# Latent attention after a dilated stage: where the heads' keys are loaded, who makes the branch pieces, when gates are stored, and the place of one copy

## The chip, the cores and the metric

The kernel runs on one core of one Trainium2 chip. The metric is the time of one execution on the device in microseconds (us); lower is better. Three runs of the kernel before gave 1240.01, 1243.35 and 1243.78 us, median 1243.35. One further execution was taken by the profiler: 1242.97 us, of which the span from the first to the last instruction is 1240.9.

## The reference

One layer of an encoder over 1024 tokens of width 1024, all in float32. Two mixers read one input projection, each is multiplied by SiLU of a branch of its own and projected, sigmoid gates weigh the two, and an output projection, a residual and a norm end it. Cut to what matters here:

```python
proj = rmsnorm(x, attn_norm_g) @ w_in     # c_q c_kv k_rope z_mla | q k v z_dil | g_mla g_dil
a_out = mla_attention(c_q, c_kv, k_rope, ...)        # 8 heads, dense, softmax over 1024 keys
y_mla = (a_out * silu(z_mla)) @ w_o_mla
d_out = dilated_mixture(q_dil, k_dil, v_dil, ...)    # 3 groups of 8 heads, dilations 1, 4, 16
y_dil = (d_out * silu(z_dil)) @ w_o_dil              # d_out: groups weighted by their softmax denominators
merged = sigmoid(g_mla + b) * y_mla + sigmoid(g_dil + b) * y_dil
out = rmsnorm(x + merged @ w_out)
```

## The kernel before

Every product of two float32 matrices is made from parts: an operand is split into a high part, rounded to the type fp32r, and a low part (the value less the high part), and three matmuls (`mm3`, lines 145 to 147: high by high, high by low, low by high) are summed. `split` (lines 151 and 152) rounds on ScalarE and subtracts on the engine that it is given, mostly GpSimd.

The program has five stages: the latent and value projections, the other projections of the dilated mixer (products of blocks), the dilated attention, the latent attention, and the output. In the last three the order of all instructions is written out by hand: every engine does its own in the order of the program, and waits by semaphores on the others. All DMAs go out through SyncE's queue (`dma`, line 141), in the program's order too: one that must wait holds up those behind it.

**Dilated attention** (`attention`). 72 units in a row, four pairs of heads with 16 units of the first two groups and 2 units of classes (the third group) each. In step t the units near t are each in another phase: scores, maxima, exponentials, transposes, values, copy, result. The last phase of a class unit (`result`, line 1255) copies its values from PSUM (tile `left`) to SBUF on VectorE. `combine` gives the steps that weigh the three groups of a pair: denominators go to DRAM and back by token, factors are made on GpSimd and VectorE (lines 1398 to 1419), stored (`s_rr`), and spread over 128 partitions by DMA (`spreads`, which uses the ring of buffers `bc`); lines 1441 and 1445 then multiply and add. For the last pair these steps fall into the first ticks of the latent attention (`LAST_STEPS`).

**Filler.** Beside all this TensorE computes the projections of the gates (`gate_fill`, 32 jobs of 8 steps, one `mm3` per step) and later those of the two branches (`proj_fill`). `feed(n)` adds n to what is owed and takes so many whole steps; in the dilated stage it is called twice per unit with `DIL_FEED`, by the group of the unit two ahead. After the last unit the steps are filled up to 224 of 256 in one go. The rest comes in the first 33 ticks of the latent attention, 2 per tick in two of four ticks. From `one_bank` on, a job has one PSUM bank.

A finished job goes through `after`: VectorE multiplies by a row factor (line 729), ScalarE takes tanh (line 735), and the tile (`zt`) joins the list `stores`; in the next jobs' third step (`kc == 2`) `store()` sends off one tile (`s_gt`). Its buffer, one of a small ring, can be written again when the store has landed. With two banks a tile joins the list after the next job's store, so it is sent a job later; this backlog of one stays when `one_bank` begins.

**Latent attention** (`mla_attention`). 32 units (head, quarter of the queries) of four ticks, c = 0 to 3. A tick transposes (line 871) the unit's exponentials, which ScalarE rounds (line 873) and VectorE subtracts (line 879). Ticks 0 and 1 make the next unit's scores (tiles `right`, `left`) and maxima (line 855); ticks 1 and 2 its exponentials (line 863). The values' matmuls (lines 895, 896) follow a tick behind; two units share a PSUM bank, whose halves ScalarE copies (line 902) and VectorE adds (line 911, `mla_sum`) before the next unit's values may write it.

At the end of every second unit of an odd head, `mla_spread` (tick c = 0) turns the denominators round (line 925), takes their reciprocals, stores them (`s_mr`) and reads them back spread over the partitions; `mla_gated` (line 941, GpSimd, tick c = 3) multiplies them into the branch's z, and `mla_weighted` (line 948, VectorE, the next unit's tick c = 1) applies both. The head after next has its queries and keys loaded (`mla_load_qk`: five DMAs, 1.5 MB, into one of two buffers each) in tick c = 1, as soon as the last scores of this head are issued, which is in the unit before its last.

`piece` makes the operands of the dilated branch's projection, eight pieces of 128 x 512 in ticks 6 to 32: the DMAs of z and of the summed dilated output y, `product` (line 1015, y = y * z on GpSimd) and a tick later `parts`, a `split` of y with the subtraction on GpSimd.

Some names are short in the profile: `at_r` and `at_f` are all tiles placed by hand (fp32r and float32), `bank` the PSUM banks, `w_h` and `w_l` the parts of weights, POOL is GpSimd, ACT ScalarE, DVE VectorE, PE TensorE, SPq SyncE's queue.

Of the kernel before, what the change touches and what calls it, by code (L numbers as in the profile page):

```python
# [10 lines left out]
F32 = mybir.dt.float32  # L11
# [3 lines left out]
ALU = mybir.AluOpType  # L15
# [13 lines left out]


FIRST_FEED = 9
DIL_FEED = (1.26, 1.26, 2.3, 1.8)

LAST_JOBS = [(dt, 0) for dt in range(4)] + [(dt + i, half) for dt in (4, 6) for half in range(2) for i in range(2)] + [(dt, 1) for dt in range(4)]
LAST_STEPS = {3: 4, 4: 6, 5: 8, 6: 9, 8: 14, 9: 15, 10: 17, 11: 19, 12: 20}
# [26 lines left out]
class Net:  # L62
# [656 lines left out]
    def gate_fill(self):  # L719
# [23 lines left out]
        for n, i in enumerate(ZG):  # L743
            w = self.split_weights.pop(n)
            for half in range(2):
                next(tail, None)
                ps = self.get("pj")
                t = slice(half * 512, half * 512 + 512)
                for kc in range(8):
                    self.mm3(ps, *self.at(w, kc), self.hTh[:, kc, t], self.hTl[:, kc, t], kc == 0, kc == 7)  # L750
                    if half == 0 and kc == 0:
                        self.weights_load(n + 2)
                    if half == 0 and kc == 4:
                        self.weights_split(n + 1)
                    if kc == 2:
                        store()
                    if kc % 2 and kc < 7:
                        next(tail, None)
                    if kc < 7:
                        yield  # L760
                run_all(tail)
                tail = after(2 * n + half, i, half, ps)
                if self.one_bank:
                    next(tail)
                yield True
# [193 lines left out]
    def mla_tick(self, k, c):  # L959

        self.mla_transposes(k, c)
        if c == 0:
            self.mla_low(k, c)
            self.mla_scores(k + 1, 0)
            self.mla_values(k - 1, 3)
            self.mla_copied(k - 1)
            self.mla_spread(k)
            self.mla_maxima(k + 1, 0)
            self.mla_sum(k - 1)
            h, u = self.units[k - 1] if k else (0, 0)  # L970
            if u == 3 and h < 6:
                self.mla_load_v(h + 2)
        elif c == 1:
            self.mla_exponentials(k + 1, 0)
            self.mla_low(k, c)
            self.mla_scores(k + 1, 1)
            self.mla_values(k, 0)
            self.mla_maxima(k + 1, 1)
            self.mla_weighted(k - 1)
            h, u = self.units[k + 1] if k + 1 < 32 else (7, 3)  # L980
            if u == 3 and h < 6:
                self.mla_load_qk(h + 2)
        else:
            if c == 2:
                self.mla_exponentials(k + 1, 1)
            self.mla_low(k, c)
            self.feed(self.rate)
            self.mla_values(k, c - 1)
            if c == 2:
                for n in {6: (), 7: (), 8: (5,), 9: (7,)}.get(k, (k - 1,)):  # L990
                    self.mla_merged(n, self.nc.gpsimd)
            else:
                self.mla_gated(k)

    def mla_attention(self, later, first):
# [5 lines left out]
        def piece(t, j, half, gap=5):  # L1001
# [10 lines left out]
                    o["y"] = self.last_sum[0][:, x]  # L1012

            def product():
                nc.gpsimd.tensor_tensor(out=o["y"], in0=o["y"], in1=o["z"], op=ALU.mult)

            def parts():
                self.split(o["y"], self.brd[0][j][half], self.brd[1][j][half], nc.gpsimd)
            put(t, load)
            put(t + gap, product)  # L1020
            put(t + gap + 1, parts)
# [281 lines left out]
    def attention(self):  # L1303
# [13 lines left out]
        for t in range(-2, N + 2):  # L1317
# [11 lines left out]
                self.mla_exponentials(0, t - N - 1) if t > N else None  # L1329
            self.feed(DIL_FEED[g])  # L1330
            do(t - 2, 6)
            do(t - 2, 7)
            if t == N + 1:
                self.places["s_mla"] = self.places["s_mla"] + self.banks_of("left", 1, S)
                self.mla_scores(0, 1)
# [4 lines left out]
            if t == N:  # L1340
# [3 lines left out]
                self.one_bank = True  # L1344
                self.places["s_mla"] = self.banks_of("right", 1, S)
                self.mla_scores(0, 0)
                self.mla_maxima(0, 0)
            if 1 <= t <= N:
                last = units[t - 1][-1]
# [388 lines left out]
```

## Time and profile before

| | |
|---|---|
| profiled execution, its span | 1242.97 us, 1240.9 us |
| median of three runs | 1243.35 us |
| TensorE matmul busy | 1206.6 us, 97% of the span |
| VectorE, ScalarE, GpSimd busy | 729.7, 616.0, 568.8 us |
| dilated attention | about 536 to 812 us of the span |
| latent attention | about 812 to 1112 us |

A row of the timeline gives the start from the span's first instruction, the duration, engine, line, operation, output and inputs, and in brackets how long the engine stood idle before it and what ended that. A row of the windows view gives for a stretch its length, then the busy time and number of instructions of PE, PE's weight loads, DVE, ACT and POOL, the granted TensorE clock, the DMA engines' share and GB/s. Other engines' idle time costs nothing as long as TensorE does not wait for them.

### The profile page before, as it was taken

Reading aid. Unit: us, or ns where it says so; the run is one execution under the profiler, and the core shown is the slowest. Engines: PE = TensorE matmul, PEld = TensorE weight load, DVE = VectorE, ACT = ScalarE, POOL = GpSimd, SP = SyncE. Lnnn points to the kernel's source line nnn. Section 1 sums busy time; section 2 is a strip of 40 time slices with the busy share of each in tenths; the row PEclk is TensorE's granted clock in tenths of the full one; section 3 lists DMA queues with packets and bytes.
Section 4 is the critical chain, followed back from the end, with each engine's and each line's share of the span. In section 5 each row is a group of like instructions: output and inputs, shape, how many; then the busy total and the mean of one; then the engine's idle time right before and its main releaser. Section 6 shows DMA issues by size and latency. Waiting matters only on the chain.

```text
span 1240.9 us, 19482 instructions
## 1 busy us (share of the span) xinstructions
PE 1206.6 (97%) x6909; PEld 1060.0 (85%) x6909; DVE 729.7 (59%) x1304; ACT 616.0 (50%) x1292; POOL 568.8 (46%) x482
## 2 busy tenths in 40 slices
PE   8989999999999999999999999999989999999997
PEld 8988999788888888888988888877878888888886
DVE  7473524466666663246566666556657767769542
ACT  7533345444343444456565656545655656654232
POOL 1361218777777777633465533415520201168322
PEclk9999999999999999999999999999999999999999
DMA  9858579365536643297889898946543445235241
GB/s 342 222 158 303 200 289 316 102 165 158 148 115 166 183 119 127 84 265 216 246 249 268 230 269 213 283 123 162 162 124 106 111 120 140 82 109 172 85 153 51
DMA packets 126416, 221.37 MB, mean 178 GB/s; under 512 B 28072, under 2 KB 60400, under 8 KB 121392
## 3 DMA queue, kind: packets, MB, share of 16 engines
q1 hardware_dynamic: 126320, 220.14, 59.8%
q8 instruction: 54, 0.88, 0.3%
q14 instruction: 42, 0.34, 0.1%
HBM read 149.24 MB, written 70.85 MB: 177 GB/s over the span
## 4 chain that ended last, share of the span: by engine, by line
PE 71%; DMA 9%; POOL 4%; issue 2%; ACT 2%; DVE 2%; SPq 1%; ACTq 0%; POOLq 0%; DVEq 0%
PE bank L145 6%; PE bank L146 6%; PE bank L147 6%; PE bank L871 3%; PE st_a L145 2%; PE st_a L147 2%; PE st_a L146 2%; PE st_d L145 2%; PE st_c L145 2%; PE st_d L147 2%; PE st_c L147 2%; PE st_c L146 2%; PE st_d L146 2%; PE bank L896 2%; PE right L145 2%
## 5 line engine op out<-in xcount | busy, mean ns | idle before, releaser
L152 POOL TENSOR_TENSOR w_l<-w_raw,w_h 128x512 fp32r<-128x512 f32 x188 | 246.1, 1322 | 231.0 <-ACT w_h L151 180.8
L151 ACT CAST w_h<-w_raw 128x512 fp32r<-128x512 f32 x188 | 112.1, 621 | 106.5 <-POOL w_raw L496 90.7
L145 PE MATMUL bank<-at_r,w_h 128*128 128x512 f32 x344 | 141.7, 412 | 0.0
L879 DVE TENSOR_TENSOR at_r<-bank,at_r 128x512 fp32r<-128x512 f32 x128 | 88.0, 688 | 82.6 <-ACT at_r L873 82.2
L146 PE MATMUL bank<-at_r,w_h 128*128 128x512 f32 x344 | 134.9, 392 | 0.6 <-POOL at_r L152 0.6
L147 PE MATMUL bank<-at_r,w_l 128*128 128x512 f32 x344 | 135.1, 393 | 0.0
L873 ACT CAST at_r<-bank 128x512 fp32r<-128x512 f32 x128 | 74.9, 586 | 75.5 <-PE bank L871 74.8
L145 PE MATMUL pj<-w_h,at_r 128*128 128x256 f32 x384 | 109.0, 284 | 0.2 <-ACT dv_s L457 0.2
L146 PE MATMUL pj<-w_l,at_r 128*128 128x256 f32 x384 | 108.9, 284 | 0.0
L147 PE MATMUL pj<-w_h,at_r 128*128 128x256 f32 x384 | 108.9, 284 | 0.0
L496 POOL TENSOR_TENSOR w_raw<-w_raw 128x512 f32<-128x512 f32 x64 | 82.9, 1295 | 0.1
L871 PE MATMUL bank<-consts,at_f 128*128 128x128 f32 x512 | 77.4, 273 | 1.6 <-ACT at_f L863 1.1
L147 PEld LDWEIGHTS bank<-at_r,w_l 128*128 128x128 f32 x344 | 64.7, 188 | 14.6
L1143 DVE TENSOR_TENSOR at_r<-bank,at_r 128x512 fp32r<-128x512 f32 x64 | 44.0, 688 | 54.4 <-ACT at_r L1139 54.2
L145 PEld LDWEIGHTS pj<-w_h,at_r 128*128 128x128 f32 x384 | 73.4, 191 | 1.3 <-ACT dv_s L457 0.6
L147 PEld LDWEIGHTS pj<-w_h,at_r 128*128 128x128 f32 x384 | 73.4, 191 | 1.0
L146 PEld LDWEIGHTS pj<-w_l,at_r 128*128 128x128 f32 x384 | 73.4, 191 | 0.7
L895 PE MATMUL bank<-at_r,at_r 128*128 128x256 f32 x256 | 67.7, 285 | 6.4 <-DVE at_f L911 3.3
L146 PEld LDWEIGHTS bank<-at_r,w_h 128*128 128x128 f32 x344 | 65.1, 189 | 9.7 <-POOL at_r L152 1.0
L145 PEld LDWEIGHTS bank<-at_r,w_h 128*128 128x128 f32 x344 | 65.1, 189 | 8.8
L896 PE MATMUL bank<-at_r,at_r 128*128 128x256 f32 x256 | 67.5, 285 | 0.9 <-DVE at_r L879 0.9
L1124 ACT ACTIVATE at_f<-at_f,at_f 128x256 f32<-128x256 f32 x128 | 64.1, 504 | 3.0 <-DVE at_f L1117 3.0
(323 smaller groups left out, 3321.6 us busy)
## 6 DMA issues: line engine op xcount, KB each, us to landing
w_raw<-wt SPq DMA_DIRECT2D x48, 512.0 KB, 4.2
at_r<-s_dq SPq DMA_DIRECT2D x32, 512.0 KB, 8.9
s_dk<-dq_st SPq DMA_DIRECT2D x80, 128.0 KB, 2.3
s_dv<-dv_st SPq DMA_DIRECT2D x32, 256.0 KB, 3.0
s_dq<-dq_st SPq DMA_DIRECT2D x64, 128.0 KB, 2.4
zt<-s_gt SPq DMA_DIRECT2D x32, 256.0 KB, 3.1
w_raw<-wv SPq DMA_DIRECT2D x12, 512.0 KB, 6.3
at_r<-s_dk SPq DMA_DIRECT2D x8, 576.0 KB, 10.1
```

The source lines that it names most:

```text
L145: mm(out, lh, rh, start=start, stop=False, skip_group_check=skip)
L146: mm(out, lh, rl, start=False, stop=False, skip_group_check=skip)
L147: return mm(out, ll, rh, start=False, stop=stop, skip_group_check=skip)
L151: self.nc.scalar.copy(out=h, in_=raw)
L152: sub.tensor_tensor(out=l, in0=raw, in1=h.bitcast(F32), op=ALU.subtract)
L496: self.nc.gpsimd.tensor_tensor(out=b[out], in0=b[x], in1=b[y], op=ALU.subtract)
L871: self.nc.tensor.transpose(pt[:, o:o + 128], self.P[k, b][:, 128 * kc:128 * kc + 128], self.ident)
L873: self.nc.scalar.copy(out=h, in_=pt)
L879: self.nc.vector.tensor_tensor(out=l, in0=pt, in1=h.bitcast(F32), op=ALU.subtract)
L895: mm(out, vv[:, kc], ph[:, x], start=kc == 0, stop=False)
L896: mm(out, vv[:, kc], pl[:, x], start=False, stop=kc == 7)
L1124: nc.scalar.activation(out=p, in_=p, func=AF.Exp, scale=-1.0, bias=nm, accum_out=den)
```

## The change

- `DIL_FEED` for the first two groups falls from 1.26 to 1.235.
- While a job has one bank, `store()` is also called in a job's sixth step (`kc == 5`).
- A head's queries and keys are loaded in tick c = 1 of the last unit of the head two before, one unit (four ticks) later; where that unit has an `mla_spread`, its DMAs now come first in the queue.
- A piece's high part is made by GpSimd: the product is computed twice, once into the fp32r operand and once in place, and the low part is the in-place product less the operand, in the next tick. ScalarE has no part in it.
- The last class unit's `result` moves from the step after the last unit, behind the first latent maxima, to the step before, between the first scores and the first maxima.

```diff
-DIL_FEED = (1.26, 1.26, 2.3, 1.8)
+DIL_FEED = (1.235, 1.235, 2.3, 1.8)
...
-                    if kc == 2:
+                    if kc == 2 or kc == 5 and self.one_bank:
                         store()
...
             self.mla_weighted(k - 1)
-            h, u = self.units[k + 1] if k + 1 < 32 else (7, 3)
+            h, u = self.units[k]
             if u == 3 and h < 6:
                 self.mla_load_qk(h + 2)
...
             def product():
-                nc.gpsimd.tensor_tensor(out=o["y"], in0=o["y"], in1=o["z"], op=ALU.mult)
+                for out in (self.brd[0][j][half], o["y"]):
+                    nc.gpsimd.tensor_tensor(out=out, in0=o["y"], in1=o["z"], op=ALU.mult)
 
             def parts():
-                self.split(o["y"], self.brd[0][j][half], self.brd[1][j][half], nc.gpsimd)
+                nc.gpsimd.tensor_tensor(out=self.brd[1][j][half], in0=o["y"], in1=self.brd[0][j][half].bitcast(F32), op=ALU.subtract)
...
             do(t - 2, 6)
-            do(t - 2, 7)
+            if t <= N:
+                do(t - 2, 7)
             if t == N + 1:
...
                 self.mla_scores(0, 0)
+                do(N - 1, 7)
                 self.mla_maxima(0, 0)
```

## The prediction

> **What bounds the kernel now.** I read the page first, then the busy time by stretches, then TensorE's waits and the timeline where it waits.
>
> ```profile
> span 1240.9 us, 19482 instructions
> PE 1206.6 (97%) x6909; PEld 1060.0 (85%) x6909; DVE 729.7 (59%) x1304; ACT 616.0 (50%) x1292; POOL 568.8 (46%) x482
> ```
> ```profile
> 536.00:800.00 264.00, 261.05 (x1661) 233.82 (x1660) 165.93 (x430) 157.67 (x421) 123.12 (x123) 1.00 0.89 247
> 800.00:835.00 35.00, 33.05 (x188) 28.16 (x187) 17.45 (x23) 15.10 (x27) 4.98 (x8) 1.00 0.55 156
> 835.00:870.00 35.00, 31.98 (x194) 27.77 (x194) 21.78 (x29) 19.69 (x36) 19.56 (x20) 1.00 0.61 153
> 870.00:910.00 40.00, 36.00 (x209) 30.33 (x208) 23.69 (x31) 22.79 (x41) 19.16 (x16) 0.98 0.54 156
> 910.00:1060.00 150.00, 150.00 (x926) 133.42 (x924) 108.29 (x139) 89.17 (x159) 20.49 (x16) 0.99 0.43 115
> ```
>
> TensorE is the bound: 1206.6 of 1240.9 us. The change removes no matmul, so it can only win what TensorE loses to waits. The second figure of a stretch, against the first, shows that: 2.95 us idle in nearly the whole dilated stage, none from 910 to 1060, but 1.95, 3.02 and 4.00 us in the 110 us between, where the latent attention begins and all five edits act. TensorE's waits in 800 to 912 name the releasers, and the timeline the places:
>
> ```profile
> PE bank L895 <- DVE at_f L911: 3.3, 3, 2.0
> PE bank L895 <- ACT at_r L873: 2.9, 1, 2.9
> PE bank L896 <- DVE at_r L879: 0.7, 2, 0.3
> ```
> ```profile
> 815.96 0.47 PE L145 MATMUL left<-at_r 96*128 96x512 f32 x1 [0.83 <-DVE at_f L1255]
> 820.21 0.55 PE L871 MATMUL bank<-consts,at_f 128*128 128x128 f32 x3 [1.12 <-ACT at_f L863]
> ...
> 840.37 0.60 PE L871 MATMUL bank<-consts,at_f 128*128 128x128 f32 x4
> ...
> 844.91 0.60 PE L871 MATMUL bank<-consts,at_f 128*128 128x128 f32 x4
> ...
> 861.02 0.60 PE L871 MATMUL bank<-consts,at_f 128*128 128x128 f32 x4
> ...
> 864.63 0.60 PE L871 MATMUL bank<-consts,at_f 128*128 128x128 f32 x4
> ```
> ```profile
> 903.43 0.60 PE L871 MATMUL bank<-consts,at_f 128*128 128x128 f32 x4
> ...
> 915.49 0.60 PE L871 MATMUL bank<-consts,at_f 128*128 128x128 f32 x4
> ```
>
> Line 871 opens a tick, so it is a clock for TensorE's progress. From 844.91 to 861.02 lie seven ticks: 16.11 / 7 = 2.30 us for a tick without a wait. By that measure tick 9 (840.37 to 844.91) loses 2.24 us, tick 17 (861.02 to 864.63) 1.31, ticks 18 to 33 (864.63 to 903.43, sixteen) 38.80 - 36.80 = 2.00, and ticks 34 to 36 (903.43 to 915.49) 12.06 - 6.90 = 5.16. Ahead of tick 1 come waits of 0.83 and 1.12 us. All of it: 12.66 us.
>
> The last 5.16 is more than the wait in it:
>
> ```profile
> 908.00:910.00 2.00, 1.34 (x5) 1.11 (x6) 1.67 (x2) 1.88 (x4) 0.41 (x1) 0.64 0.64 240
> 910.00:912.00 2.00, 2.00 (x9) 1.72 (x7) 1.35 (x3) 1.81 (x4) 0.02 (x1) 0.51 0.55 169
> ```
>
> The granted clock (third figure from the end) is 0.64 and 0.51 after the idle time; I price this stall by its ticks. The Trainium skill, "TensorE: Matmul & The Clock Gate", "What's actually happening", has the half clock come after an idle window of about 3.4 us; a wait of 2.9 us would by that keep the full clock, and the term would be 2.9 in place of 5.16. The trace differs, and the measurement decides.
>
> **The change, part by part.**
>
> *The last class result before the first maxima.*
>
> ```profile
> 813.66 1.23 DVE L855 TENSOR_REDUCE m_nm<-right 128x1 f32<-128x1024 f32 x1 [0.77 <-PE right L147]
> 814.81 1.01 DVE L1255 COPY at_f<-left 128x512 f32<-128x512 f32 x1
> 861.00 0.69 DVE L729 TENSOR_TENSOR zt<-bank,at_f 128x512 f32<-128x512 f32 x1 [2.58 <-DMA s_gt<-zt]
> ```
>
> The copy of 1.01 us ends at 815.82, and TensorE's scores into the bank that it frees start at 815.96. It stood behind the maximum of 813.66, before which VectorE was idle for 0.77 us waiting for scores. In front of that maximum the copy runs from 812.89 to 813.90, before TensorE asks at 815.13 (815.96 less its wait). The 0.83 us go. The maximum starts 0.24 us later, and with it an exponential on ScalarE; its reader comes only behind two stretches of filler, so this costs nothing.
>
> *Feed.* The steps of the dilated stage were 9 + 64 x 2.52 + 11 x 4.6 + 3.6 = 224, just the mark to which they are filled up; with 1.235 they are 9 + 64 x 2.47 + 11 x 4.6 + 3.6 = 221. So three steps go from the 64 units to the place right before the first tick. A step is three matmuls:
>
> ```profile
> 817.43 0.39 PE L145 MATMUL bank<-at_r,w_h 128*128 128x512 f32 x1
> 818.13 0.39 PE L145 MATMUL bank<-at_r,w_h 128*128 128x512 f32 x1
> ```
>
> 0.70 us each, 2.1 in all, in front of the wait of 1.12 us for the first exponentials: it goes. Cover is lost in the dilated stage, 0.03 us per unit, where TensorE's idle time is 2.95 us in 264. Bounds: if loads set the pace there (DMA engines 0.89 busy) all 2.1 us come back as waits; if the shifted jobs happen to close one of the waits, 0.8 us are won. I take 0.3, near the small end, as only three or four places wait at all.
>
> *Pieces on GpSimd alone.* In ticks 6 to 32 ScalarE, which rounds every tick's transposes, stood in its queue behind casts of pieces that waited for GpSimd:
>
> ```profile
> 840.73 0.62 ACT L151 CAST at_r<-zt 128x512 fp32r<-128x512 f32 x1 [3.35 <-POOL zt L1015]
> ...
> 906.45 0.62 ACT L151 CAST at_r<-zt 128x512 fp32r<-128x512 f32 x1 [5.08 <-POOL zt L1015]
> ```
> ```profile
> 839.42 1.28 POOL L1015 TENSOR_TENSOR zt<-zt,at_f 128x512 f32<-128x512 f32 x1
> ...
> 843.16 1.25 POOL L1015 TENSOR_TENSOR zt<-zt,at_f 128x512 f32<-128x512 f32 x1
> ...
> 903.90 1.29 POOL L941 TENSOR_TENSOR at_f<-at_f 128x512 f32<-128x512 f32 x1 [5.20 <-DMA at_f<-s_mr]
> ```
>
> The cast at 840.73 is the root of tick 9: the rounding (L873), VectorE's subtraction, a maximum and the sum L911 follow it in their queues, and TensorE's values wait for L911. The cast at 906.45 is the root of tick 34: it waited for a product that stood behind the gating L941, which waited for `s_mr`. Without the casts these 2.24 and 5.16 us go, and of the 2.00 in ticks 18 to 33, where the same casts and stores delay L879 and L911, I count 1.8 (two of these ticks hold one more transpose on TensorE, L925).
>
> Added are eight products of 1.28 us on GpSimd, 10.2 us, less eight casts of 0.62 us, 5.0 us, on ScalarE. GpSimd is busy 19.56 of 35 and 19.16 of 40 us there, so it has room; what counts is who stands behind. At 839 to 846 its operations are back to back, and behind them in SyncE's queue are the spreads of the last pair's factors, since they overwrite the buffers from which the second product reads:
>
> ```profile
> 844.44 3.65 SPq L141 DMA_DIRECT2D at_f<-s_rr  x6
> ...
> 851.39 0.34 SPq L141 DMA_DIRECT2D s_gt<-zt  x1
> ```
> ```profile
> 846.21 5.16 DMA at_f<-s_rr
> ```
> ```profile
> 856.05 1.28 DVE L1441 TENSOR_TENSOR at_f<-at_f 128x512 f32<-128x512 f32 x2
> ```
> ```profile
> DMA to landing us min/median/max: 2.3/6.0/11.5
> ```
>
> The last row is for another DMA, the last part of a head's keys (`s_kp`). Today the spreads start when that product ends (843.16 + 1.25), and the fourth has landed at 851.37, 4.68 us before its reader on VectorE at 856.05. Two more products come ahead of it (2.56 us), and TensorE's ticks, which set the reader's place, come 2.24 us sooner against GpSimd: 4.80 us of 4.68. So VectorE waits 0.1 us if the DMA takes 5.16 as now. Bounds: nothing, or, with that part's longest landing in place of 5.16, 6.3 us. I take 0.5, by the same DMA's own row.
>
> *Stores a job sooner.* The tile at 851.39 was sent a job late, behind the heads' load; VectorE waited for its landing until 861.00, and tick 17's 1.31 us are that. With the backlog gone the tile is sent some eight ticks earlier: the 1.31 go. The additional DMA issue on SyncE's queue, 0.34 us, only moves.
>
> *Keys behind the spread.*
>
> ```profile
> 886.45 0.45 SPq L141 DMA_DIRECT2D at_r<-s_qn  x1
> ...
> 893.16 0.29 SPq L141 DMA_DIRECT2D s_mr<-at_f  x1
> ...
> 900.39 1.09 SPq L141 DMA_DIRECT2D at_f<-s_mr  x2
> ```
>
> `s_mr` was issued at 893.16 behind a head's queries and keys, and its readers had to wait for its landing until 900.39. In the new order it is issued with the queue empty. This is the other half of tick 34 and adds no term, but it keeps VectorE's L948, which needs L941 too, from taking over the stall. A head's load then comes 15 ticks before its first scores, 7 for the last head:
>
> ```profile
> 1038.05 0.27 SPq L141 DMA_DIRECT2D s_mr<-at_f  x1
> ```
> ```profile
> 1053.05 0.47 PE L145 MATMUL right<-at_r 96*128 96x512 f32 x1
> ```
>
> Behind the spread of 1038.05, with its two readers and five issues of about half a microsecond, the last part is issued near 1042.5 (estimate from the rows' issue times) and, by the 6.0 and 11.5 above, lands at 1048.5 at the median, 1054 at the worst; it is needed at 1053.05. I take 0, bound 1.
>
> *Sum.* 0.83 + 1.12 + 2.24 + 1.31 + 1.8 + 5.16 = 12.46 us removed; 0.3 + 0.5 come back, and I keep 0.3 for small waits that no row shows. Gain 11.4: 1242.97 - 11.4 = 1231.6 for a profiled execution. The median of the runs is 0.38 above the profiled one, so 1232.0.
>
> **The rivals.**
>
> 1. *The spreads take the casts' place.* VectorE waits in tick 14 or 15 for a spread that lands as late as the bound, 6.3 us, of which TensorE, which uses VectorE's results a tick later, sees 6.3 - 2.3 = 4, and a microsecond more by the low clock. For: 4.80 against 4.68. Against: the same DMA took 5.16. Gain 11.4 - 5 = 6.4: 1237.
> 2. *VectorE keeps the stalls.* GpSimd's queue, longer by 10.2 us, delays L941 so that L948 on VectorE stands where the cast stood: the 5.16 from tick 34 on stay, 11.4 - 5.2 = 6.2: 1237. Against: GpSimd is half idle, and L941 waited for `s_mr`, not for work.
> 3. *GpSimd and VectorE block each other.* Six operations of VectorE with two inputs from SBUF (L1441 four times, L948 twice) fall among the added products; if each is held for one of 1.28 us, 7.7 us come back, 11.4 - 7.7 = 3.7: 1239.6. The row at 856.05 speaks against it: two of them took 0.64 each. By the Trainium skill, "SBUF — State Buffer", "SBUF: two separate sides", a two-input VectorE operation and a GpSimd operation lock a shared port against each other for a whole instruction, which would be this case; the trace of before shows no such hold in that row.
> 4. *No change.* The releasers that the profile infers are not the true ones, and the waits only move: 1243.
> 5. *Slower: the keys' burst.* Four heads' loads now come after the gates' loads of the second projection have begun, and push gate tiles and values behind them. If each costs TensorE a stall such as tick 34's, 11.4 - 4 x 5.16 = -9.2: 1252.6. It decides where a burst lands later than the work that needs it, for the last head beyond 10.5 us after issue. Against: the burst was in that stage before too, four ticks earlier, and 910 to 1060 has no idle time.
>
> **How the numbers follow.** Forecast 0.68 (1229.5 to 1235), rivals 1 to 5: 0.11, 0.07, 0.05, 0.05, 0.04. A measurement of this kernel tells about 0.3%, 3.7 us, from no change; forecast and rivals 1 and 2 are faster by more, rival 3 about half: 0.88. The rest of it and rival 4 are the same: 0.08; slower 0.04. The range: at the low end all 12.66 us and 0.8 of the feed go, 1243.35 - 13.46 = 1229.9, and I leave 0.4 below it, the distance of the profiled run from the median: 1229.5. At the high end rivals 1 and 2 are in: 1237.5.
>
> **What would show it.** Right: 800 to 910 with under 1 us idle in place of 8.97; line 871 every 2.30 us from tick 1 to 36; granted clock 1.00 throughout; no ScalarE cast of line 151 from `zt` or `at_f` before tick 34; `s_mr` read within 2 us of its issue. Wrong: L1441 waiting for `at_f<-s_rr` with TensorE behind it, a wait for `at_r<-s_kn` or `s_kp` near the last head's first scores, or new idle time before 800.

## The result, and the profile after

The kernel after took 1228.93 us in the median of six runs (1226.29 to 1231.00), the kernel before 1243.57 in six (1240.01 to 1248.18, the three named at the start among them): a ratio of 0.987, 95% interval 0.985 to 0.990. Its profiled execution took 1229.1 us, 13.9 us less than that of before, where 11.4 were forecast.

The first two lines of the page after, and the stretches that the prediction showed (columns as there):

```profile
span 1227.1 us, 19477 instructions
PE 1204.8 (98%) x6909; PEld 1061.2 (86%) x6909; DVE 729.4 (59%) x1304; ACT 611.9 (50%) x1284; POOL 579.1 (47%) x490
```
```profile
536.00:800.00 264.00, 263.41 (x1674) 235.69 (x1673) 167.18 (x433) 159.82 (x425) 122.92 (x123) 1.00 0.89 249
800.00:835.00 35.00, 35.00 (x204) 30.40 (x203) 19.32 (x25) 15.65 (x29) 9.90 (x14) 1.00 0.48 144
835.00:870.00 35.00, 34.99 (x214) 30.66 (x213) 24.23 (x31) 20.77 (x37) 22.40 (x20) 1.00 0.66 174
870.00:910.00 40.00, 38.83 (x237) 34.09 (x236) 27.31 (x36) 22.32 (x40) 24.96 (x20) 1.00 0.61 172
910.00:1060.00 150.00, 150.00 (x932) 133.44 (x931) 108.53 (x140) 88.70 (x158) 20.45 (x16) 1.00 0.42 108
```

TensorE's idle time from 800 to 910 is 1.18 us in place of 8.97. That was the forecast. The first row was not: 0.59 us idle in the dilated stage, where 2.95 were and a little more was expected.

The clock of line 871, from the timeline of after (first rows of some ticks):

```profile
816.85 0.60 PE L871 MATMUL bank<-consts,at_f 128*128 128x128 f32 x4
...
860.56 0.60 PE L871 MATMUL bank<-consts,at_f 128*128 128x128 f32 x4
863.27 0.66 PE L871 MATMUL bank<-consts,at_f 128*128 128x128 f32 x4
...
900.29 0.60 PE L871 MATMUL bank<-consts,at_f 128*128 128x128 f32 x4
904.03 0.60 PE L871 MATMUL bank<-consts,at_f 128*128 128x128 f32 x4
```

From tick 1 to the start of tick 37 are 83.44 us, 36 ticks of 2.30 and 0.64 of waits; before it were 93.51, so 10.07 us are gone. Two ticks are still long. Tick 20 (860.56 to 863.27) loses 0.41, tick 37 (900.29 to 904.03) 1.44. VectorE's and SyncE's rows of after show why:

```profile
861.32 0.69 DVE L1444 TENSOR_TENSOR at_f<-at_f,at_f 128x512 f32<-128x512 f32 x1 [3.21 <-DMA at_f<-s_rr]
...
902.23 0.69 DVE L811 SCALAR_TENSOR_TENSOR at_f<-zt,bank 128x512 f32<-128x512 f32 x1 [4.34 <-DMA zt<-s_gt]
```
```profile
885.36 0.31 SPq L141 DMA_DIRECT2D s_mr<-at_f  x1
887.88 1.09 SPq L141 DMA_DIRECT2D at_f<-s_mr  x2
889.07 0.55 SPq L141 DMA_DIRECT2D at_r<-s_qn  x1
...
891.24 0.58 SPq L141 DMA_DIRECT2D at_r<-s_kp  x1
...
892.99 9.88 SPq L141 DMA_DIRECT2D zt<-s_gt  x4
```

In tick 20 it is one of the last pair's spreads (the prediction's rival 1, at 0.41 of the 5 us that it feared). In tick 37 it is a gate tile that was asked for at 892.99, right behind a head's load of 1.5 MB, and read by line 811 at 902.23: rival 5, in one place of the four that it feared.

Of the signs that the prediction named for being right, three were narrowly missed: 1.18 us idle from 800 to 910 where under 1 was asked, a long tick 20 among the 36, and `s_mr` read 2.5 us behind its issue where 2 was asked.

Where the 13.8 us between the two spans (1240.9 and 1227.1) lie. The dilated stage is counted from its first score to the first line 871, the latent attention from there to its last:

| | before | after | difference |
|---|---|---|---|
| ahead of the dilated stage | 537.9 | 537.3 | -0.6 |
| dilated stage | 280.90 | 277.70 | -3.20 |
| latent attention | 293.24 | 283.26 | -9.98 |
| rest | 128.86 | 128.85 | 0 |

The first row is scatter: no instruction there is changed, and the profiled executions below have 533.1 to 540.5. It is also what makes single times of this kernel differ by several us, so that most of what follows is read from stages and ticks, and the runs' medians stand beside it.

### The profile page after: what moved, and what is told of

It reads as the page before. It is cut to its first block, busy times and chain, and to the rows that moved or that the text cites. A ratio compares the mean times of both kernels' runs of the same rounds, so it can differ in the third digit from the quotient of the medians.

```text
span 1227.1 us, 19477 instructions
## 1 busy us (share of the span) xinstructions
PE 1204.8 (98%) x6909; PEld 1061.2 (86%) x6909; DVE 729.4 (59%) x1304; ACT 611.9 (50%) x1284; POOL 579.1 (47%) x490
## 4 chain that ended last, share of the span: by engine, by line
PE 78%; DMA 9%; DVE 3%; ACT 3%; POOL 3%; issue 2%; SPq 1%; ACTq 0%; POOLq 0%; DVEq 0%
PE bank L145 6%; PE bank L147 6%; PE bank L146 6%; PE bank L871 4%; PE st_a L145 2%; PE st_a L147 2%; PE st_a L146 2%; PE st_c L146 2%; PE st_d L146 2%; PE st_d L145 2%; PE st_c L145 2%; PE st_d L147 2%; PE st_c L147 2%; PE bank L896 2%; PE bank L895 2%
```

## The experiments

A tick's loss is its length, from line 871 to line 871, less 2.30 us; those of before are in the prediction (tick 9 2.24, tick 17 1.31, ticks 18 to 33 2.00, ticks 34 to 36 5.16). The feed is 1.235 in a kernel that is made from after and 1.26 in one made from before, unless told otherwise. Ratios are to runs of the kernel before on the same chip.

### The feed

`feed_only` is the kernel before with

```diff
-DIL_FEED = (1.26, 1.26, 2.3, 1.8)
+DIL_FEED = (1.235, 1.235, 2.3, 1.8)
```

> The kernel before with the lower feed alone. Theory A (the feed shifts the filler against the DMA landings of the dilated stage and so closes waits there): the 1.12 us wait before the first tick goes and the idle time from 536 to 800 falls from 2.95 to about 0.6 us, 3.5 us less in all: about 1240 against 1243.6, with the 0.83 us wait for the last class copy and the stalls from tick 9 on unchanged. Theory B (those waits of the dilated stage come and go between executions, whatever the feed): only the 1.12 us go, about 1242.5, idle time from 536 to 800 anywhere between 0.5 and 3. Theory C (my prediction's term): the idle time there grows by 0.3 us, 1242.8.

1239.12 us, ratio 0.998 (0.996 to 1.000). Waits of 2.1 us are left in the dilated stage, 0.85 less than before, where theory A has 2.4 less. The ticks lose 11.5 us, without tick 17's but with 1.4 in tick 10: behind tick 9's wait of 1.94 us the granted clock was 0.50 for 3.4 us.

```profile
838.38:841.79 3.41, 3.41 (x14) 2.93 (x13) 2.38 (x3) 3.08 (x6) 1.27 (x1) 0.50 0.60 166
```

`all_but_feed` is the kernel after with

```diff
-DIL_FEED = (1.235, 1.235, 2.3, 1.8)
+DIL_FEED = (1.26, 1.26, 2.3, 1.8)
```

> The changed kernel with the feed of before. Theory A: the idle time from 536 to 800 is about 3 us again and the wait before the first tick returns, so 3.5 us above the changed kernel's 1228.9: 1232.4. Theory B: 1230.1, with an idle time from 536 to 800 that does not follow the feed. Theory C: 1229.7.

1233.53 us, ratio 0.994 (0.991 to 0.997). Waits of 3.38 us in the dilated stage, which lasts 282.66 us; the wait of 1.1 us before the first tick is back.

`first_feed_6` has that edit and three filler steps fewer ahead of the units, the old rate shifted:

```diff
-FIRST_FEED = 9
+FIRST_FEED = 6
```

> The changed kernel with the feed of before, but 6 instead of 9 steps ahead of the first unit: as many steps reach the place before the first tick, the units have the old cover each, and every job ends three steps later in the units, as it does near the end with the lower feed. If the place of the steps against the units decides (phase), the idle time from 536 to 800 is under 1 us and the time that of the changed kernel, 1228.9; if the smaller cover per unit decides, it is near 3 us and the time 1231.3. If the waits come and go by themselves it lies within 1 us of the changed kernel with an idle time that no pattern gives.

1236.04 us, ratio 0.995 (0.993 to 0.998). The shift takes away the two waits of 1.26 that are named below the table and brings others (1.55 us at 8 us from the stage's start, 0.62 at 115, 1.69 at 170): 5.27 us in all. So the waits changed places, as phase has it, but not to under 1 us, as the expectation had it. Behind the waits of 1.55 and 1.69 us the granted clock was 0.50 for 3.4 us each:

```profile
544.81:548.22 3.41, 3.41 (x9) 2.53 (x8) 1.37 (x5) 1.08 (x5) 3.22 (x3) 0.50 0.84 211
705.23:708.64 3.41, 3.41 (x12) 3.02 (x13) 1.63 (x7) 2.61 (x8) 1.41 (x2) 0.50 1.05 248
```

`feed_1245` and `feed_1225` are the kernel after with two other values:

```diff
-DIL_FEED = (1.235, 1.235, 2.3, 1.8)
+DIL_FEED = (1.245, 1.245, 2.3, 1.8)
...
-DIL_FEED = (1.235, 1.235, 2.3, 1.8)
+DIL_FEED = (1.225, 1.225, 2.3, 1.8)
```

> The kernel after with a feed of 1.245 in place of 1.235 (1.26 before). If the feed counts through the places at which gate jobs end against the units (phase), the waits in the dilated stage come and go with the value, in no order: with 1.245 some other places wait, between 0.5 and 3.5 us in all, and no wait of 0.75 us at 193 to 194 together with one of 1.5 us at 248 to 249 us behind the stage's start. If it counts through the amount (cover), 1.245 lies between 0.6 us (1.235) and 3 us (1.26) and waits at the same two places. Either way 1229 to 1232 us.

1229.6 us, ratio 0.988 (0.985 to 0.991); waits of 1.13 us in the dilated stage. Ticks 37 and 38 lose 3.7 us here (1.44 in after): TensorE's wait there was 1.85 us (1.17 in after), and the granted clock behind it 0.50 for 3.4 us (1.00 in after).

> The kernel after with a feed of 1.225 in place of 1.235. Four steps fewer than at 1.26 stand between the units, one or two more before the first tick. Phase: waits somewhere between 0.5 and 3.5 us in the dilated stage. Amount, with less better: 0.6 us or under, the time at or below that of 1.235. The prediction's view, by which less filler is less cover: 0.7 us or more. 1228 to 1232 us.

1234.47 us, ratio 0.992 (0.989 to 0.994); waits of 1.74 us, one of 1.37 us at 163, and 1.80 us more in the steps in front of the first tick, where TensorE waits for line 729 to clear the job's bank.

`feed_result` is the kernel before with two edits:

```diff
-DIL_FEED = (1.26, 1.26, 2.3, 1.8)
+DIL_FEED = (1.235, 1.235, 2.3, 1.8)
...
-            do(t - 2, 7)
+            if t <= N:
+                do(t - 2, 7)
...
                 self.mla_scores(0, 0)
+                do(N - 1, 7)
```

> The kernel before with two edits, the feed of 1.235 and the last class result in front of the first maxima. If the feed's value sets the waits in the dilated stage: under 1.2 us there, no wait of 0.75 us at 193 us or of 1.5 us at 248 us, none at the class copy, 1.12 us less before the first tick, and the ticks' 10 us of waits as in the kernel before: about 1243.4 - 2.4 - 0.8 - 1.1 = 1239 us. If they go with the execution: 1 to 4 us in the dilated stage at other places than in the run with the feed alone, and 1240 to 1242 us.

1237.6 us, ratio 0.994 (0.991 to 0.996): 0.36 us of waits in the dilated stage, none of the old ones. The ticks lose 11.7 us, 1.0 more than before.

Since no other edit touches the dilated stage, every kernel is an execution of it with its feed. Waits up to 262 us from its start, and its length:

| feed | executions | waits, us | length, us |
|---|---|---|---|
| 1.26 | 3 (before, `all_but_feed`, `pieces_only`) | 1.96 to 3.38 | 280.90 to 282.81 |
| 1.245 | 1 | 1.13 | 278.15 |
| 1.235 | 12 (after, and eleven below and above) | 0.35 to 2.10, ten under 1 | 276.37 to 280.55, eleven under 278.7 |
| 1.225 | 1 | 1.74 | 280.25 |

The lengths of 1.26 and 1.235 don't overlap, if only by 0.35 us (`feed_only` is the longest of 1.235), the waits only by one execution (again `feed_only`, which waits 1.06 us at 98 us from the stage's start, where the others have at most 0.46): the gain goes with the value. Two of the lengths at 1.26 include a low clock: behind the longer wait of the stage it was 0.50 for 3.4 us in `all_but_feed` and for 6.8 us in `pieces_only`, while it was 1.00 there in before and in all executions of 1.235. That the gain does not go with the amount is shown only in part: the one execution each of 1.245 and 1.225 waits more than ten of the twelve at 1.235, but less than the longest of them. It weighs more that `first_feed_6`, with the rate of 1.26 and its jobs shifted, waits at other places. At 1.26 TensorE waits 1.50 to 1.62 us at 246 to 249 us from the stage's start in all three, and 0.75 to 0.80 at 193 to 194 in two; at 1.235 no execution has over 0.36 us at the one or over 0.34 at the other. Here is the longer wait, ScalarE's rows and TensorE's, in before and in `all_but_feed`:

```profile
783.70 0.72 ACT L735 ACTIVATE zt<-zt,consts 128x512 f32<-128x512 f32 x1 [3.83 <-DVE zt L729]
784.33 0.57 ACT L1139 CAST at_r<-bank 128x512 fp32r<-128x512 f32 x1
784.79 0.51 ACT L1124 ACTIVATE at_f<-at_f,at_f 128x256 f32<-128x256 f32 x1
...
785.45 0.33 PE L1131 MATMUL bank<-consts,at_f 128*128 128x128 f32 x1 [1.50 <-ACT at_f L1124]
```
```profile
787.53 0.72 ACT L735 ACTIVATE zt<-zt,consts 128x512 f32<-128x512 f32 x1 [3.89 <-DVE zt L729]
788.16 0.57 ACT L1140 CAST at_r<-bank 128x512 fp32r<-128x512 f32 x1
788.62 0.51 ACT L1125 ACTIVATE at_f<-at_f,at_f 128x256 f32<-128x256 f32 x1
...
789.28 0.33 PE L1132 MATMUL bank<-consts,at_f 128*128 128x128 f32 x1 [1.62 <-ACT at_f L1125]
```

A gate job ends just there. Its tanh (line 735) waits 3.8 us for VectorE's line 729, and behind it in ScalarE's queue stand a rounding and the exponentials for which TensorE waits. In after (the same stretch, lines shifted by one):

```profile
779.82 0.51 ACT L1125 ACTIVATE at_f<-at_f,at_f 128x256 f32<-128x256 f32 x1 [1.24 <-DVE at_f L1118]
...
780.48 0.33 PE L1132 MATMUL bank<-consts,at_f 128*128 128x128 f32 x1 [0.26 <-ACT at_f L1125]
...
784.95 0.72 ACT L735 ACTIVATE zt<-zt,consts 128x512 f32<-128x512 f32 x1 [3.43 <-DVE zt L729]
```

The tanh still waits 3.43 us, but now behind the exponentials that TensorE needs first, which cost it 0.26. The value of the feed sets at which place of a unit a job ends. That the waits at these two places come and go with the value is shown by the runs; that the tanh in front makes the wait of 1.50 is read from the traces and was not tried by itself.

### The pieces

`all_but_pieces` is the kernel after with `product` and `parts` as before:

```diff
-                for out in (self.brd[0][j][half], o["y"]):
-                    nc.gpsimd.tensor_tensor(out=out, in0=o["y"], in1=o["z"], op=ALU.mult)
+                nc.gpsimd.tensor_tensor(out=o["y"], in0=o["y"], in1=o["z"], op=ALU.mult)
...
-                nc.gpsimd.tensor_tensor(out=self.brd[1][j][half], in0=o["y"], in1=self.brd[0][j][half].bitcast(F32), op=ALU.subtract)
+                self.split(o["y"], self.brd[0][j][half], self.brd[1][j][half], nc.gpsimd)
```

> The changed kernel with the pieces' high parts cast on ScalarE again. Measured from the first to the last tick in the profile (283.3 us in the changed kernel, 293.2 before), which leaves out the scatter of the earlier stages. Theory A (a cast stalls ScalarE only as long as GpSimd's product is late; with the keys behind the spread GpSimd no longer waits for s_mr): the stall of tick 9 returns (2.2 us) and some of ticks 25 to 27 (0.7 us), not that of tick 34: 286.2. Theory B (the casts alone make all three): 2.2 + 1.2 + 5.2 come back, 291.9.

1229.94 us, ratio 0.992 (0.988 to 0.995). Tick 9 loses 2.25 again and ticks 25 to 27 1.17, but tick 34 only 0.13: with the spread's read landed early, the product that the last casts wait for is early too. From the first to the last line 871 are 285.3 us, near theory A's 286.2 and 2.1 more than in after, which the medians can't show (tick 37 loses only 0.23 here).

`pieces_only` is the kernel before with the same lines the other way round, the change's edit of the pieces and nothing else.

> The kernel before with the pieces alone on GpSimd. Theory A: tick 9's 2.25 us and most of the 2.0 us in ticks 18 to 33 go, but tick 34 stays near its 4 us in another form, since the gating on GpSimd still waits for the spread behind the load and VectorE's product waits for that: 1243.4 - 4 = about 1239.5 us. Theory B (the casts are the root of tick 34, as the prediction had it): 1243.4 - 9.2 = 1234 us. For the feed of 1.26: waits of about 0.75 us at 193 to 194 us and 1.5 us at 248 to 249 us behind the stage's start if they go with the value, others or none if with the execution.

1246.05 us, ratio 1.001 (0.999 to 1.004): nothing is won, which neither theory had. Tick 9 is short and ticks 18 to 32 nearly all, as expected, but ticks 17 and 18 lose 8.2 us in place of 1.3, and 33 and 34 4.2, there too by line 729 behind a store (3.69 us at 906.29). SyncE's, VectorE's and TensorE's rows of `pieces_only`:

```profile
848.13 3.65 SPq L141 DMA_DIRECT2D at_f<-s_rr  x6
851.87 0.54 SPq L141 DMA_DIRECT2D at_r<-s_qn  x1
...
854.88 0.39 SPq L141 DMA_DIRECT2D s_gt<-zt  x1
```
```profile
864.07 0.69 DVE L729 TENSOR_TENSOR zt<-bank,at_f 128x512 f32<-128x512 f32 x1 [6.95 <-DMA s_gt<-zt]
...
867.13 0.58 PE L895 MATMUL bank<-at_r,at_r 128*128 128x256 f32 x1 [5.46 <-DVE at_f L911]
```

The spreads wait for GpSimd's second product and go out at 848.13 (844.44 before), the head's load behind them, and behind that the gate's store at 854.88 (851.39 before). Its landing frees the tile that line 729 writes, at 864.07 (861.00 before), while tick 17 begins sooner (859.7, before 861.02). In the kernel after no such wait is left, and undoing either the stores or the keys (below) doesn't bring it back: either of the two is enough here, and without both the pieces don't pay. Both take the store that line 729 needs out from behind the load. In `all_but_stores` it goes out just ahead of it:

```profile
840.30 0.58 SPq L141 DMA_DIRECT2D s_gt<-zt  x1
840.93 0.44 SPq L141 DMA_DIRECT2D at_r<-s_qn  x1
```

In `all_but_keys` a store still goes out behind the load (847.56, landed at 856.52), but line 729 runs at 849.06 without it: what it needs had been sent by 820.86.

Is it the cast on ScalarE that costs, or its wait for GpSimd? Three kernels keep the casts on ScalarE but two ticks later. `late_casts` is `all_but_pieces` with

```diff
-            put(t + gap + 1, parts)
+            put(t + gap + 3, parts)
```

In all three, some pieces are cast from a buffer that a later load has already filled again, so that the branch's projection gets other data; the work is of the same amount.

> The kernel after, with the pieces' high parts cast on ScalarE again as before, but two ticks later, so that GpSimd's product has long been made when the cast's turn comes. Theory A (what cost TensorE time was that the cast waited 3.35 to 5.08 us for GpSimd at the head of ScalarE's queue, not the cast itself): the eight casts of 0.62 us show waits of ScalarE well under 1 us, tick 9 stays under 0.2 us of excess, ticks 18 to 33 under 0.5 us in all, and the time is that of the kernel after, 1228 to 1231 us. Theory B (the 0.62 us on ScalarE is the cost, wherever it stands): 1 to 2 us of excess in the ticks of the casts, 1231 to 1233 us.

1235.79 us, ratio 0.994 (0.993 to 0.996). Up to tick 35 theory A holds: tick 9 loses nothing, ticks 18 to 33 lose 0.66, a little over the 0.5 expected. But ticks 36 and 37 lose 8.8: the last piece's cast stood 8.02 us in ScalarE's queue for a load of gates into its own buffer, which the edit itself put in front of it.

`late_casts_keys` has in addition the load of `keys_after_gates` (below).

> The casts on ScalarE two ticks later, and the load of head 3 behind the gates' loads (as in the run that put it there). With GpSimd's eight second products gone, the last pair's spreads are issued earlier, so that the wait of tick 20 (0.3 to 0.7 us) goes; with the load later, that of tick 37 (1.4 us) goes. If both hold and nothing else waits, the latent attention's ticks lose under 0.5 us in all and the time is 1.5 to 2 us under the kernel after: 1227 us. If the casts' 0.62 us on ScalarE show in the ticks, the gain is lost again: 1229 us or more.

1233.63 us, ratio 0.992 (0.990 to 0.995). Tick 20's wait is gone (0.11), ticks 36 to 38 lose 5.0 by the same cast (4.15 us in its queue).

`six_late_keys` is `late_casts_keys` with the last two pieces made by GpSimd alone, as in after, and in their old ticks:

```diff
-            put(t + gap + 3, parts)
+            put(t + gap + (3 if t < 24 else 1), parts)
```

> The kernel after, with the first six pieces' high parts cast on ScalarE two ticks later, the last two left on GpSimd, and head 3's load behind the gates' loads. Theory A (only the wait for GpSimd cost time, and GpSimd's second products delay the last pair's spreads): no excess over 0.5 us in any tick from 1 to 40, since tick 20's wait for a spread goes with the earlier issue and tick 37's for gates with the later load: 1.5 us under the kernel after, about 1227.5 us. Theory B (the cast costs by itself): 1 to 2 us of excess in ticks 9 to 28, 1229 us or more. For the feed: the dilated stage at 1.235 has under 1 us of waits if the waits go with the value, anything up to 4 us if they go with the execution.

1227.54 us, ratio 0.987 (0.984 to 0.989). The only ticks with a loss are 20, 25 and 28 (0.11, 0.43, 0.11): theory A. The time stands 1.4 us under that of after, within what the two sets of runs can tell apart.

`early_products` is `all_but_pieces` with the load of `keys_after_gates` and the products a tick earlier (for the last pair, j = 3, the casts a tick later), so that each cast comes two ticks behind its product and ahead of the load that takes its buffer:

```diff
-            put(t + gap, product)
-            put(t + gap + 1, parts)
+            put(t + gap - (j < 3), product)
+            put(t + gap + 1 + (j == 3), parts)
```

> The kernel after, with the pieces' high parts cast on ScalarE in the ticks of the kernel before, GpSimd's single product a tick earlier (for the last pair's two pieces the cast a tick later instead), and head 3's load behind the gates' loads. Theory A (only the wait at the head of ScalarE's queue cost time): the casts wait under 1 us, ticks 1 to 40 lose under 1.2 us in all, against 2.0 in the kernel after and 10.5 in the kernel before, and the time is 1 to 1.5 us under the kernel after, about 1227.5 us. Theory B (the casts cost by themselves, or the products in their new place delay the spreads as the second products did): 2 us or more in ticks 9 to 28, 1230 us or more.

1229.21 us, ratio 0.988 (0.985 to 0.991): no different from the kernel after. Tick 9 loses nothing, tick 26 1.53. ScalarE's rows of the second and the fifth piece:

```profile
837.20 0.62 ACT L151 CAST at_r<-zt 128x512 fp32r<-128x512 f32 x1 [0.85 <-POOL zt L1018]
...
876.42 0.62 ACT L151 CAST at_r<-zt 128x512 fp32r<-128x512 f32 x1 [3.16 <-POOL at_r L152]
```

Where the cast waits 0.85 us TensorE loses nothing; where it waits 3.16, until the end of a subtraction that stands behind the product and the gating in GpSimd's queue, the tick is long. It is the wait at the head of ScalarE's queue that costs, not the 0.62 us, but for a small rest: tick 25 loses 0.28 to 0.43 us in all eight kernels that cast pieces on ScalarE and nothing in the ten others, for a reason that no run shows. The forecast of at most 1.2 us for these ticks was missed by one cast (2.2 measured).

### The keys

`all_but_keys` is the kernel after with

```diff
-            h, u = self.units[k]
+            h, u = self.units[k + 1] if k + 1 < 32 else (7, 3)
```

> The changed kernel with a head's keys loaded in the unit before the last, as before. Theory A (as the prediction put it: without the casts the late s_mr stops VectorE's L948 instead, so the keys' place guards what the pieces won): L948 waits some 2 us in tick 33, TensorE 1 to 2 us behind it, while the 1.4 us of tick 37 go: 283 to 284.5 from the first to the last tick. Theory B (the keys' place is what ended the stall of tick 34): 5.2 us come back, 287 to 288.5. Theory C (the keys' place gives nothing): 281.9, faster than the changed kernel.

1233.63 us, ratio 0.993 (0.989 to 0.996). GpSimd's and VectorE's rows:

```profile
897.02 1.26 POOL L941 TENSOR_TENSOR at_f<-at_f 128x512 f32<-128x512 f32 x1 [10.93 <-DMA at_f<-s_mr]
...
898.32 1.73 DVE L948 TENSOR_TENSOR at_f<-at_f 128x512 f32<-128x512 f32 x1 [4.76 <-POOL at_f L941]
```

Ticks 35 and 36 lose 6.9 us, and from the first to the last line 871 are 289.1 us: theory A's mechanism, at more than theory B's size. The gating waits for the spread behind the load, and now VectorE's line 948 stands where ScalarE's cast stood: rival 2's mechanism, kept away by the keys. Of TensorE's one wait of 4.30 us there, 1.05 come from what held line 948 (last section), and the granted clock was 0.50 from 899.8 to 906.7.

`keys_after_gates` is the kernel after with head 3's load moved on, behind the gates' first loads:

```diff
-            if u == 3 and h < 6:
+            if u == 3 and h < 6 and h != 1:
                 self.mla_load_v(h + 2)
...
-            if u == 3 and h < 6:
+            if u == 3 and h < 6 and h != 1:
                 self.mla_load_qk(h + 2)
...
+            if k == 8 and c == 2:
+                self.mla_load_qk(3)
+                self.mla_load_v(3)
```

> The changed kernel with head 3's queries, keys and values loaded behind the first gate tiles of the second projection instead of in front of them (tick 34 instead of 29). If the new wait in tick 37 is the gate tile standing behind the head's load, VectorE's 4.3 us wait for it falls under 1 us and TensorE's 1.4 us in tick 37 go: 1227.5. If the gate tile is late for another reason (its buffer's store), nothing changes: 1228.9.

1229.68 us, ratio 0.989 (0.986 to 0.993). The stretch of tick 37's wait in after, and the same stretch in `keys_after_gates`:

```profile
902.00:904.00 2.00, 0.83 (x6) 0.51 (x5) 1.77 (x3) 0.00 (x0) 0.00 (x0) 1.00 0.54 205
```
```profile
902.00:904.00 2.00, 2.00 (x15) 1.78 (x14) 1.60 (x3) 1.52 (x3) 0.00 (x0) 1.00 1.12 287
```

Tick 37 loses nothing: the burst ahead of the gates' loads was its cause. The ticks gain 1.1 us, which the median of the runs can't show.

### The stores

`all_but_stores` is the kernel after with

```diff
-                    if kc == 2 or kc == 5 and self.one_bank:
+                    if kc == 2:
```

> The changed kernel without the second place of the stores. Theory A (the store was late because it stood behind the heads' load; with the load after it in the queue it lands in time): VectorE's wait for it in tick 15 is under 0.5 us and nothing comes back, 283.3 from the first to the last tick. Theory B (it is late by the job alone): the 1.3 us of tick 17 and the half microsecond of tick 33 come back, 285.1.

1232.96 us, ratio 0.993 (0.990 to 0.995). Tick 17 stays short, against the prediction's term. Ticks 37 and 38 lose 6.8 us instead, and from the first to the last line 871 are 288.7 us, which neither theory had. SyncE's and VectorE's rows:

```profile
887.25 0.43 SPq L141 DMA_DIRECT2D at_r<-s_mv  x1
887.78 1.15 SPq L141 DMA_DIRECT2D s_gt<-zt  x2
897.17 1.90 SPq L141 DMA_DIRECT2D zt<-s_gt  x4
```
```profile
899.83 0.69 DVE L811 SCALAR_TENSOR_TENSOR at_f<-zt,bank 128x512 f32<-128x512 f32 x1 [7.34 <-DMA zt<-s_gt]
```

The backlog's last two gate tiles go out together behind the head's load, and the gates' first loads can go out only at 897.17 (892.99 in after).

### The class result

`all_but_result` is the kernel after with

```diff
-            if t <= N:
-                do(t - 2, 7)
+            do(t - 2, 7)
...
-                do(N - 1, 7)
```

> The changed kernel with the last class result behind the first maxima again. Theory A: TensorE's wait of 0.8 us for that copy returns and nothing else: 0.8 us above the changed kernel, the first to the last tick unchanged at 283.3. Theory B (with three more steps of filler behind it, the wait is only shortened by later work): nothing returns.

1228.6 us, ratio 0.990 (0.987 to 0.993): no different. In its profile TensorE waits 1.18 us for the last class copy (line 1256 there), and the ticks are as in after: theory A, at a size that the medians can't show.

## Why the prediction came out as it did

The direction, the bound and most of the mechanism were right: TensorE's waits in the 110 us where the latent attention begins go, and nothing else becomes the bound. The gain was 13.8 us of span and not 11.4. **The step that failed is the feed's term in the part on the change**: "I take 0.3, near the small end, as only three or four places wait at all". The sign was wrong. The dilated stage became 3.20 us shorter, 0.83 of it by the class result, so the feed won 2.4 (its waits fell from 2.95 to 0.59). The argument priced cover, a quantity that falls with the feed; by the runs the waits go with the place at which jobs end, and so the three or four waits, two of them long, could go altogether. The bound of 0.8 us on that side was too small as well: it allowed one wait of a middling size to close, where the trace of before held one of 1.50. Why just 1.235 meets nearly no wait is not shown.

Point by point:

- **The wait for the last class copy**, 0.83: gone, and back (1.18) when the move was undone.
- **The wait before the first tick**, 1.12: gone at 1.235 (the first tick takes 1.83 us, 3.16 before) and back at 1.26.
- **Ticks 9, 17, 18 to 33 and 34 to 36**, 10.51 forecast, 10.07 measured with what came back in ticks 20 and 28. The sum came out near, but the owners were partly wrong, so it was safe only because all five edits went in together. Tick 9 and ticks 18 to 33 belong to the pieces. Tick 34's 5.16 was booked to the pieces, with the keys adding "no term"; undoing the pieces brought back 0.13 of it and undoing the keys 6.9. Tick 17's 1.31 was booked to the stores; undoing them did not bring it back, with the feed alone it is missing, and with the feed and the class result it is 1.61. In `feed_only` the store goes out as late behind the start of tick 9 as in before (11.2 us, 11.0 before), but TensorE came 1.4 us later by the low clock of tick 10. In the kernel after, the stores or the keys suffice, each without the other.
- **Give-backs**: 0.5 for the spreads, 0.41 measured, which is near by luck: it is another spread than the fourth, and tick 20 loses 0.11 to 0.71 in the ten kernels with the second products. In tick 37 1.44 where 0.3 was kept for small waits: the gate tiles behind the burst.
- **The last head's load**: asked for a bound of 1, cost nothing. Its last part, issued at 1028.92 in after, landed 9.8 us later, at 1038.7, and the first score that needs it starts at 1039.27, so 0.5 us are left.

With these the sum is 0.83 + 1.33 + 10.07 - 1.44 + 2.37, and 0.6 of scatter ahead of the stage: 13.8.

Of the rivals, the first and the fifth happened, at 0.41 and 1.44 us. The second did not, because of the keys. The fourth did not for the change as a whole, but `pieces_only` is a case of it: the wait moves to the next thing in the queue. The third happened on VectorE, for three of the six operations and at 0.2 to 0.3 us each, since GpSimd's operation was more than half done when each began (last section): the two of 1.28 us at 856.05 in before took 1.47 in after, and line 948 took 1.01 and 0.94 where 0.68 is usual. No tick of TensorE is longer for it. The row of 856.05, which the forecast set against this rival, could not tell: no GpSimd operation was running when its two began; the next started at 856.88.

On the clock: `pieces_only` has a wait of 5.46 us, and in its next two stretches of 2 and 6 us the clock was

```profile
868.00:870.00 2.00, 2.00 (x9) 1.81 (x9) 1.49 (x3) 0.70 (x2) 1.09 (x1) 0.50 0.66 140
870.00:876.00 6.00, 6.00 (x30) 5.27 (x29) 1.90 (x3) 2.61 (x5) 4.41 (x4) 0.76 0.62 218
```

This is why a tick behind such a wait is long too (1.97 us for tick 18). After tick 37's wait in after, 1.2 us, it stayed at 1.00. By the Trainium skill, "TensorE: Matmul & The Clock Gate", "What's actually happening", the half clock comes after about 3.4 us of idle time; the 5.46 and the 1.2 agree with that, the 2.9 us before with 0.64 and 0.51 do not, so the forecast was right to price that stall by its ticks. Nor do the shorter waits above, of 1.55 to 1.94 us, behind which the clock was 0.50 for 3.4 or 6.8 us in `first_feed_6`, `pieces_only`, `all_but_feed`, `feed_1245` and `feed_only`; behind the waits of 1.50 and 1.97 us at 785.45 and 844.33 in before it stayed at 1.00. So here a wait from about 1.5 us on may cost more than its length, and that varies from one execution to the next (tick 10 of `feed_only`: 1.4 us).

## What to carry to other kernels

Price edits in a hand-ordered pipeline as a set: here the pieces alone won nothing, because one queue hands a delay on to the next user, and each edit's worth depended on the others. A wait at the head of an in-order queue costs what stands behind it, so ask of every instruction whether its input is there when its turn comes, before counting its own time. Where filler is spread over a periodic pipeline, its rate is a choice of phase; try two or three values on the chip, since the amount of cover tells neither sign nor size.

## What was not expected of the hardware

In `all_but_keys` line 948, with both inputs in SBUF, took 1.73 us (its row is above) where 0.68 is usual. It began at 898.32, just behind the start of one of GpSimd's products; below are that product, and then the same pair and GpSimd's next operation in after:

```profile
898.24 1.26 POOL L1016 TENSOR_TENSOR at_r<-zt,at_f 128x512 fp32r<-128x512 f32 x1
```
```profile
893.94 1.29 POOL L1016 TENSOR_TENSOR zt<-zt,at_f 128x512 f32<-128x512 f32 x1
895.31 1.62 POOL L1019 TENSOR_TENSOR at_r<-zt,at_r 128x512 fp32r<-128x512 f32 x1
...
894.85 0.94 DVE L948 TENSOR_TENSOR at_f<-at_f 128x512 f32<-128x512 f32 x1
```

In both, line 948 ends 0.55 us behind the end of the GpSimd operation that was running when it began (899.50 and 900.05, 895.23 and 895.79): it was held until that one was done, for 1.05 us where it came at its start and for 0.26 us where it came late. GpSimd's next operation, which began while line 948 ran, took 1.62 us in place of about 1.3. The 18 traces agree: of such operations on 128 x 512 elements (line 948, line 1441 and the same lines shifted), 114 began while an operation of GpSimd of that size ran, and 111 of them end 0.55 to 0.61 us behind it (three were held through a second one); the 248 without one beside them took 0.66 to 0.69 us. The Trainium skill, "SBUF — State Buffer", "SBUF: two separate sides", says that such a pair lock each other out for a whole instruction; these rows agree.

The other surprise was how much a small store suffers behind a burst: `s_mr`, stored at 885.36 in after with no head's load ahead of it, could be read back from 887.88 on, 2.5 us later (1.2 to 2.3 at its other stores in after); stored at 893.16 in before, behind a head's load, only from 900.39 on, 7.2 us later.
